# A conditioning map moved out of the FFNs into the first attention stage, with its scores spread

## The chip, the cores and the metric

The kernel runs on one core of one Trainium2 chip. The time is the device time of one execution in microseconds (us), smaller is better; a verdict compares the medians of runs. The engines that appear below: PE multiplies matrices, PEld loads its stationary operand, DVE, ACT and POOL work on vectors, SP issues the transfers.

## What is computed

One step of a two-layer trunk on 512 latent tokens and 128 context tokens, model width 1024. Both layers have a token mixer (layer 0: windowed attention, "mixer A"; layer 1: neighbourhood attention, "mixer B") and a gated FFN with a short convolution. In front of each of the four sub-layers the tokens are normalised and modulated by a shift and a scale, and behind it the result is gated; shift, scale and gate come from a condition vector by a linear map, one per layer:

```python
def adaln(cond, w_ada, b_ada):
    m = jax.nn.silu(cond) @ w_ada + b_ada
    return [t[:, None, :] for t in jnp.split(m, 6, axis=-1)]

    hs = modulate(rmsnorm(xs, norm_attn_w[i]), ms[0], ms[1])
    ...
    xs = xs + ms[2] * o_s
    hs = modulate(rmsnorm(xs, norm_ffn_w[i]), ms[3], ms[4])
    xs = xs + ms[5] * conv_ffn(hs, w_up[i], conv_w[i], conv_b[i], w_down[i])
```

`w_ada` is 1024 x 6144 in float32 for each layer, 25 MB. Since it depends on the condition alone, its product can be made at any time before its first use.

## The kernel before

The 640 tokens are five tiles of 128 (tile 4 is the context). Nearly every product is made in three passes of float32r halves ("hi" and "lo": an ACT copy and a subtraction, on POOL or DVE), so each weight that arrives is split first: `load_w` (line 130 the transfer, 161 the ACT copy `whi`, 164 the subtraction `wlo`).

**The conditioning map, "adaLN blocks".** Each layer's `w_ada` is cut into 12 blocks of 512 columns. A block is four transfers of 512 KB (`adst`, four buffers, so exactly one block), then two steps of the generator `ada_queue`. Its first step makes eight sums on PE (`ps_ada<-adst,cT`), copies the row out of PSUM (`adrow`: ACT, line 189, or DVE, line 191, by the flag `on_act`) and issues the next block's four transfers, which wait for these sums since they reuse the buffers. Its second step is `ada_done`: a few small PE products of `adrow` with a selection matrix, and a DVE operation into `mcol` or, for gates, a copy and a transfer to DRAM. Four of the 24 blocks are made at the start (`ada_first`). Before the change six are made in mixer A and fourteen in the FFNs: twelve in layer 0's and two in layer 1's, at the places that `ADA_UPS` lists among the 44 up-projections.

**Mixer A** runs in slots n = 3 to 20. A slot n has the scores of one pair of head group and query tile, the probability product of the pair before, and a share of the next group's projections. The order of the slot is written out as a string of letters in `SLOTS`, one for each piece: S is one head's score (two products into `ps_s`, which has two buffers, a DVE maximum with the mask, an ACT exponential `pexp`), V a step of the probability product (transposes `ps_p`, split by ACT and DVE into `ptr`, products `ps_o`), T a transposition of new queries and keys (`ps_tr`), Q a sixth-row piece of the projections (three products into `ps_mm`), O a piece of the output projection (`ps_op`), A one step of `ada_queue`. PE follows this order strictly. For the other engines and SP a scheduler places instructions within what the dependences allow; transfers on SP go out in the order so made, one queue, and one that waits holds those behind it.

**The start** follows two strings (`START`): x loads a token tile, n normalises and transposes it (`first_pre`), w loads weights, p and d are the first blocks' steps, f modulates a tile's half (`first_post`, lines 265 to 269), q a tile's projections.

**Row norms** (`norm_stat`, line 339, and `first_pre`, line 245) take the sum of squares of a row, then `rsqrt`: one DVE operation (303), logarithm and exponential on ACT (305, 308), four one-element DVE operations (310 to 313) of which three read two tensors, and a DVE multiplication of the whole row (339). They stand before each FFN: there the output projection's last tiles are normed and transposed (`ps_nt`), modulated (365, 367), split (375, 376) and fed to the first up-projections (`ps_up`). The order there is the string `OPROJ`.

**The FFN** (`ffn`) goes over 22 pairs of up-projections (`ps_up`) with convolution and gate (lines 920 to 948) and, in groups, down-projections (`ps_dn`).

Of the kernel before, what the change touches and what calls it, by code (L numbers as in the profile page):

```python
# [18 lines left out]
P = 128  # L19
# [10 lines left out]
SLOTS = {"A3": "SSQSTST", "A4": "SASATQSVTSQVQVQVQV", "A19": "SSVTSVSVTVV",  # L30
         "AT": "SOOSOOSVOSVOTVOOVTOVOOVOOSVOSVOSVOOSVOOVOOVOOSVOSVOSVOSVOOVOOOVOOVO",
         "a0": "SQSQSVTSVQTQVQVQVQVQ", "a1": "SQSQSTVSTVQTQVQVQVQVQ", "a2": "SQSQSVTSVQTQVQVQVQQ",
         "a3": "VQQTSQSVTSQSQQQQ", "a4": "QSTQSQSTSVQVQVQVQQV",
# [20 lines left out]

ADA_UPS = (0, 1, 3, 4, 6, 7, 8, 9, 11, 12, 14, 15, 17, 18, 20, 21, 23, 24, 26, 27, 29, 30, 32, 33), (0, 1, 3, 4)
# [8 lines left out]
class Trunk:  # L66
# [189 lines left out]
    def first_post(self, xT, hT, h, t, lo_eng):  # L256

        nc = self.nc
        A = self.abA[(0, 0)]
        j = 1 if t == 4 else 0  # L260
        sl = slice(t * P, (t + 1) * P)
        for c in range(4):
            f = 4 * h + c
            v = xT[h][:, c, sl]
            i = nc.vector.tensor_scalar(v, v, A[:, j, f:f + 1], self.mcol[0][:, j, f:f + 1], op0=OP.mult, op1=OP.add)
            self.tc.keep_in_program_order(i)
        v, d = xT[h][:, :, sl], [hT[p][h][:, :, sl] for p in range(2)]
        nc.scalar.activation(d[0], v, AF.Copy)  # L268
# [64 lines left out]
    def norm_stat(self, x, pool):  # L333

        nc = self.nc
        xn = pool.tile([P, D], F32, name="xn", tag="xn", bufs=self.xn_bufs)
        ss = self.sm.tile([P, 1], F32, name="nss", tag="nss")
        nc.scalar.activation(xn, x, AF.Square, accum_out=ss)
        nc.vector.tensor_scalar(xn, x, self.rsqrt(ss, 1, D), None, op0=OP.mult)  # L339
        return xn  # L340
# [585 lines left out]
    def ffn(self, l, hT, xs, groups, first, ahead, after):  # L926
# [3 lines left out]
        for gi, n in enumerate(groups):  # L930
            gh = self.ap.tile([P, 4, T], F32R, name="gh", tag="act")
            gl = self.ap.tile([P, 4, T], F32R, name="gl", tag="act")
            for k in range(n):
                zz = []
                for ff in (f + k, f + k + NF):
# [8 lines left out]
                    after("up")  # L944
# [19 lines left out]
def body(nc, tc, I, O):  # L964
    with ExitStack() as top:
# [16 lines left out]
        with ExitStack() as c1:  # L982
# [4 lines left out]
            for w in START[0].split():  # L987
# [8 lines left out]
                elif w[0] == "w":  # L996
                    W.append(k.load_w(I["wqa"][0, i], 768, k.wp, None, (sp, "load", 12)))
# [8 lines left out]
        with c2:  # L1006
            k.mp = k.pool(c2, "mixa", side="right")
            k.qT_bufs, k.pexp_bufs = 3, 4
            steps = k.ada_queue([(0, n) for n in range(4, 10)], True, "p", 3)
# [23 lines left out]
            for w in START[1].split():  # L1033
# [4 lines left out]
                elif w[0] == "f":  # L1038
                    k.first_post(xT, hT, 1, i - 10, nc.gpsimd if i > 12 else nc.vector)
# [9 lines left out]
            for n in range(3, 21):  # L1049
# [127 lines left out]
def finish_layer(k, l, wo, of, xsrc, cw):  # L1177
    nc = k.nc
    with ExitStack() as c:
        k.xp = k.pool(c, f"x{l}", side="right")  # L1180
        k.fp = k.pool(c, f"ffn{l}", side="right")
        if l == 1:
            k.adp = k.pool(c, "ada2", side="right")
# [17 lines left out]
        k.ada_next = k.ada_tiles(l, 10)  # L1201
# [115 lines left out]
        k.ffn(l, hT, xs, (4, 4, 2, 4, 4, 4), first, ahead, after)  # L1317
# [78 lines left out]
```

## Time and profile before

| what | value |
|---|---|
| median of three runs | 1751.34 us (1751.18 to 1751.69) |
| the profiled execution | 1752.72 us, of which the span 1750.9 us |
| PE busy | 1634.8 us (93%) |
| DVE, ACT, POOL busy | 894.9, 759.6, 943.5 us |
| mean granted PE clock | 0.975 |
| moved by transfers | 184.86 MB |

The durations quoted below come from that one profiled execution. A line of the timeline gives the start and the length in us, the engine, the line of the kernel, what is written and read, and in square brackets the idle time ahead of it with what ended it. A line of a table of stretches gives the stretch and its length, then each engine's busy time with its instructions in brackets, then the granted clock of PE, the busy share of the transfer engines and GB/s. A line of the waits gives who waited for whom, us in total, times, and the longest. In names of rows, line numbers are those of the kernel before.

The stages by time: the start to about 82 us; mixer A's slots 3 to 19 to 295; the rest of mixer A with the output projection to 379; layer 0's FFN to 880; mixer B to about 1225; output projection and norms to 1283; layer 1's FFN to the end.

### The profile page before, as it was taken

The page shows a single profiled execution, that of the slowest core. Times are in us where ns is not written, and L with a number is a line of the kernel's source. Part 1 is how long each engine was busy: PE and PEld are TensorE (multiplying, and loading weights), DVE is VectorE, ACT ScalarE, POOL GpSimd, SP SyncE. Part 2 cuts the span into 40 slices and gives each one's busy share as a digit, 9 for nine tenths or more (in the row PEclk, how much of TensorE's full clock was granted, in tenths as well). Part 3 has the DMA queues.
Part 4 walks back from the last instruction along what each step waited for, and adds up shares of the span by engine and source line. Part 5 has one row for each costly group of instructions (what it writes and reads, how often), then busy time and mean ns, then how long its engine had stood idle before and what let it go on. Part 6 is the DMA issues. An engine that isn't in the chain of part 4 may idle for free.

```text
span 1750.9 us, 26310 instructions
## 1 busy us (share of the span) xinstructions
PE 1634.8 (93%) x9736; PEld 1460.2 (83%) x9736; DVE 894.9 (51%) x2147; ACT 759.6 (43%) x1697; POOL 943.5 (54%) x790
## 2 busy tenths in 40 slices
PE   6798888989999999999988999998999999999998
PEld 4666776778889888899978899987789999999997
DVE  4777787673333242333475667677653232432334
ACT  4465656454132222232355777776442232323231
POOL 1544445454454573556535767776455656746461
PEclk9799998999999999999999999999999999999999
DMA  8432222425243344231222211123533222213131
GB/s 315 150 120 81 97 89 89 159 84 203 99 181 109 111 142 145 97 124 56 65 101 73 78 54 49 61 91 116 200 109 97 74 84 74 84 61 97 49 97 61
DMA packets 74592, 184.86 MB, mean 106 GB/s; under 512 B 16200, under 2 KB 25672, under 8 KB 74464
## 3 DMA queue, kind: packets, MB, share of 16 engines
q1 hardware_dynamic: 74464, 183.18, 31.2%
q8 instruction: 77, 1.26, 0.3%
q14 instruction: 51, 0.42, 0.1%
HBM read 171.32 MB, written 14.12 MB: 106 GB/s over the span
## 4 chain that ended last, share of the span: by engine, by line
PE 78%; DVE 11%; ACT 5%; DMA 2%; issue 2%; POOL 1%; SPq 0%; DVEq 0%; ACTq 0%; POOLq 0%
PE ps_up L136 35%; PE ps_dn L136 19%; PE ps_mm L136 10%; PE ps_ada L136 3%; PE ps_s L136 2%; PE ps_o L136 2%; PE ps_op L136 2%; PE ps_p L142 2%; PE ps_tr L142 1%; ACT pexp L641 1%; PE ps_nt L142 1%; DVE ps_s L636 1%; DVE xn L339 1%; DVE rs_r L313 1%; ACT whi L161 1%
## 5 line engine op out<-in xcount | busy, mean ns | idle before, releaser
L136 PE MATMUL ps_up<-hF,whi 128*128 128x320 f32 x2688 | 602.4, 311 | 5.1 <-POOL hF L376 5.1
L164 POOL TENSOR_TENSOR wlo<-wst,whi 128x1024 fp32r<-128x1024 f32 (+3 forms) x192 | 418.7, 2186 | 242.6 <-ACT whi L161 238.4
L136 PEld LDWEIGHTS ps_up<-hF,whi 128*128 128x128 f32 x2688 | 454.8, 189 | 25.4 <-issue 6.8
L136 PE MATMUL ps_up<-hF,wlo 128*128 128x320 f32 x1344 | 416.5, 311 | 0.0
L161 ACT ACTIVATE whi<-wst 128x1024 fp32r<-128x1024 f32 (+3 forms) x195 | 186.5, 962 | 437.1 <-PE ps_dn L136 160.5
L136 PEld LDWEIGHTS ps_up<-hF,wlo 128*128 128x128 f32 x1344 | 253.7, 189 | 4.9 <-issue 2.6
L922 DVE SCALAR_TENSOR_TENSOR z<-ps_up,convc,z 128x511 f32<-128x511 f32 (+1 forms) x176 | 95.8, 544 | 288.1 <-ACT z L920 284.3
L463 POOL TENSOR_TENSOR x<-x,xtmp 128x512 f32<-128x512 f32 x100 | 129.3, 1297 | 147.9 <-DVE xtmp L462 147.8
L462 DVE TENSOR_TENSOR xtmp<-ps_dn,gate 128x512 f32<-128x512 f32 x120 | 81.8, 689 | 241.7 <-PE ps_dn L136 238.8
L136 PE MATMUL ps_mm<-whi,hB 128*128 128x384 f32 x580 | 181.5, 352 | 9.5 <-DVE rs_r L327 9.5
L136 PE MATMUL ps_dn<-whi,gh 128*128 128x512 f32 x440 | 173.0, 393 | 1.8 <-DVE xtmp L462 1.6
L136 PE MATMUL ps_dn<-wlo,gh 128*128 128x512 f32 x440 | 172.2, 391 | 0.0
L136 PE MATMUL ps_dn<-whi,gl 128*128 128x512 f32 x440 | 169.8, 390 | 0.0
L136 PE MATMUL ps_mm<-whi,hA 128*128 128x384 f32 x320 | 114.5, 388 | 13.1 <-ACT hA L268 9.6
L948 POOL TENSOR_TENSOR gl<-z,gh 128x640 fp32r<-128x640 f32 x44 | 69.2, 1572 | 92.3 <-ACT gh L947 92.3
L136 PEld LDWEIGHTS ps_mm<-whi,hB 128*128 128x128 f32 x580 | 109.0, 191 | 11.7 <-ACT vb L513 8.9
L920 ACT ACTIVATE z<-ps_up,convc 128x640 f32<-128x640 f32 x88 | 76.9, 874 | 70.0 <-PE ps_up L136 69.9
L923 DVE SCALAR_TENSOR_TENSOR z<-ps_up,convc,z 128x511 f32<-128x511 f32 (+1 forms) x176 | 96.6, 549 | 5.6
L136 PE MATMUL ps_mm<-wlo,hB 128*128 128x384 f32 x290 | 98.6, 340 | 0.0
L136 PEld LDWEIGHTS ps_dn<-whi,gh 128*128 128x128 f32 x440 | 82.6, 188 | 17.8 <-DVE xtmp L462 3.5
L136 PEld LDWEIGHTS ps_dn<-whi,gl 128*128 128x128 f32 x440 | 82.3, 188 | 17.2
L136 PEld LDWEIGHTS ps_dn<-wlo,gh 128*128 128x128 f32 x440 | 82.6, 188 | 13.7
(210 smaller groups left out, 2950.1 us busy)
## 6 DMA issues: line engine op xcount, KB each, us to landing
adst<-in_wada_dram SPq DMA_DIRECT2D x96, 512.0 KB
wst<-in_wup_dram SPq DMA_DIRECT2D x78, 512.0 KB
wst<-in_wdown_dram SPq DMA_DIRECT2D x44, 512.0 KB
wst<-in_wqb_dram SPq DMA_DIRECT2D x29, 384.0 KB
wst<-in_wqa_dram SPq DMA_DIRECT2D x16, 384.0 KB
xd<-xring SPq DMA_DIRECT2D x20, 256.0 KB
x<-xd SPq DMA_DIRECT2D x10, 512.0 KB
wst<-in_woa_dram SPq DMA_DIRECT2D x8, 384.0 KB
```

The source lines that it names most:

```text
L136: i = self.nc.tensor.matmul(out, lhsT, rhs, start=start, stop=stop)
L142: i = self.nc.tensor.transpose(out, in_, idn)
L161: i = nc.scalar.activation(hi, st, AF.Copy)
L164: (lo_eng or nc.gpsimd).tensor_tensor(lo, st, _f(hi), OP.subtract)
L313: nc.vector.tensor_tensor(r, l, u, OP.mult)
L339: nc.vector.tensor_scalar(xn, x, self.rsqrt(ss, 1, D), None, op0=OP.mult)
L462: nc.vector.tensor_tensor(tmp, ps, gate[:, j, sl], OP.mult)
L463: (nc.gpsimd if pool_add else nc.vector).tensor_tensor(x[:, sl], x[:, sl], tmp, OP.add)
L920: nc.scalar.activation(z, u, AF.Identity, scale=w[:, 1:2], bias=w[:, 3:4])
L922: nc.vector.scalar_tensor_tensor(z[:, a + 1:b], u[:, a:b - 1], w[:, 0:1], z[:, a + 1:b], op0=OP.mult, op1=OP.add)
L923: nc.vector.scalar_tensor_tensor(z[:, a:b - 1], u[:, a + 1:b], w[:, 2:3], z[:, a:b - 1], op0=OP.mult, op1=OP.add)
L948: nc.gpsimd.tensor_tensor(gl[:, k], zz[0], _f(gh[:, k]), OP.subtract)
```

## The change

Three edits are made at once.

1. `ADA_UPS`, and with it every block in the FFNs, goes. Mixer A's queue now holds 20 blocks: the rest of layer 0 and all of layer 1. Each slot string has two A (one block), and the four S, which stood near the slot's front, are spread over it. All rows of these blocks are now copied by ACT.
2. In the start, the string is reordered (f03, f13 and f14 come earlier), the last two modulations of the second half go to ACT (`on_act`) with the lo part on DVE, and two weights' lo parts go from POOL to DVE.
3. The row norms use `rsqrt_row`: three one-element DVE operations that read one tensor and take the other operands as per-row scalars.

```diff
-SLOTS = {"A3": "SSQSTST", "A4": "SASATQSVTSQVQVQVQV", "A19": "SSVTSVSVTVV",
+SLOTS = {"A3": "SAQSATSTS", "A4": "SASATQVTSQVQVSQVQV", "A19": "SASATSVTSVVSVVO",
...
-         "a0": "SQSQSVTSVQTQVQVQVQVQ", "a1": "SQSQSTVSTVQTQVQVQVQVQ", "a2": "SQSQSVTSVQTQVQVQVQQ",
+         "a0": "SAQQASVQTSVQVSQTVQVQVQ", "a1": "SAQQASTVQTSVQVSTQVQVQVQ", "a2": "SAQQASVQTSVQVSQTVQVQQ",
...
-ADA_SLOTS, ADA_PLACES = (6, 9, 11, 14), (1, 3)
-START = ("... f00 f01 f02 q0 p p p p q1 n3 p p p p w2 w3 d q2 n4 f03 f04 d s1 q3 q4",
-         "f10 f11 f12 c q0 l0 l1 q1 t f13 l2 l3 q2 a f14 Q Q Q Q t t q3 A Q Q A t t q4")
+START = ("... f00 f01 f02 q0 p p p p q1 n3 f03 p p p p w2 w3 d q2 n4 f04 q3 d s1 q4",
+         "f10 f11 f12 f13 f14 c q0 l0 l1 q1 t l2 l3 q2 a Q Q Q Q t t q3 A Q Q A t t q4")
...
-ADA_UPS = (0, 1, 3, 4, 6, 7, 8, 9, 11, 12, 14, 15, 17, 18, 20, 21, 23, 24, 26, 27, 29, 30, 32, 33), (0, 1, 3, 4)
...
-        nc.vector.tensor_scalar(xn, x, self.rsqrt(ss, 1, D), None, op0=OP.mult)
+        nc.vector.tensor_scalar(xn, x, self.rsqrt_row(ss, D), None, op0=OP.mult)
...
+            sc, sh = A[:, j, f:f + 1], self.mcol[0][:, j, f:f + 1]
+            if on_act:
+                nc.scalar.activation(v, v, AF.Identity, scale=sc, bias=sh)
+            else:
+                i = nc.vector.tensor_scalar(v, v, sc, sh, op0=OP.mult, op1=OP.add)
...
+    def rsqrt_row(self, ss, d):
+        nc = self.nc
+        a, l, u, r = (self.sm.tile([P, 8], F32, name=f"rs_{v}", tag=f"rs_{v}")[:, 0:1] for v in "alur")
+        nc.vector.tensor_scalar(a, ss, 1.0 / d, EPS, op0=OP.mult, op1=OP.add)
+        i = nc.scalar.activation(l, a, AF.Ln)
...
+        nc.scalar.activation(l, l, AF.Exp, scale=-0.5)
+        nc.vector.tensor_scalar(u, l, l, a, op0=OP.mult, op1=OP.mult)
+        nc.vector.tensor_scalar(u, u, -0.5, 1.5, op0=OP.mult, op1=OP.add)
+        nc.vector.tensor_scalar(r, u, l, None, op0=OP.mult)
+        return r
...
-                    W.append(k.load_w(I["wqa"][0, i], 768, k.wp, None, (sp, "load", 12)))
+                    W.append(k.load_w(I["wqa"][0, i], 768, k.wp, nc.vector if i < 2 else None, (sp, "load", 12)))
...
-            steps = k.ada_queue([(0, n) for n in range(4, 10)], True, "p", 3)
+            steps = k.ada_queue([(0, n) for n in range(4, 12)] + [(1, n) for n in range(12)], True, "p", 3)
...
-                    k.first_post(xT, hT, 1, i - 10, nc.gpsimd if i > 12 else nc.vector)
+                    k.first_post(xT, hT, 1, i - 10, nc.vector, i > 12)
...
-        blocks = [(l, 10), (l, 11)] + [(1, n) for n in range(10) if l == 0]
-        steps = k.ada_queue(blocks, False, "dn", 2)
-        ups_done = iter(range(44))
-        def after(kind, *args):
-            if kind == "up":
-                if next(ups_done) in ADA_UPS[l]:
-                    next(steps)
-            else:
-                last(*args)
```

How this moves instructions, at three places. The first is PE in mixer A, from the first score of slot n = 10 on (`pexp` are exponentials, `hA` the modulated tokens, `adst` a block's columns, `adrow` its row). Before:

```order
L136 MATMUL ps_s<-kTa,qTa 128x512 x2
L136 MATMUL ps_mm<-whi,hA_100 128x384
L136 MATMUL ps_mm<-wlo,hA_100 128x384
L136 MATMUL ps_mm<-whi,hA_102 128x384
L136 MATMUL ps_s<-kTa,qTa 128x512 x2
L136 MATMUL ps_mm<-whi,hA_100 128x384
L136 MATMUL ps_mm<-wlo,hA_100 128x384
L136 MATMUL ps_mm<-whi,hA_102 128x384
L136 MATMUL ps_s<-kTa,qTa 128x512 x2
L142 MATMUL ps_p<-ident,pexp 128x128 x4
L142 MATMUL ps_tr<-identr,kd 128x128 x2
L136 MATMUL ps_s<-kTa,qTa 128x512 x2
```

and now:

```order
L132 MATMUL ps_s<-kTa,qTa 128x512 x2
L132 MATMUL ps_ada<-adst,cT 32x512 x8
L132 MATMUL ps_mm<-whi,hA_100 128x384
L132 MATMUL ps_mm<-wlo,hA_100 128x384
L132 MATMUL ps_mm<-whi,hA_102 128x384
L132 MATMUL ps_mm<-whi,hA_100 128x384
L132 MATMUL ps_mm<-wlo,hA_100 128x384
L132 MATMUL ps_mm<-whi,hA_102 128x384
L132 MATMUL ps_ada<-sel,adrow 128x2 x4
L132 MATMUL ps_s<-kTa,qTa 128x512 x2
L138 MATMUL ps_p<-ident,pexp 128x128 x4
```

Where four scores stood within twelve rows there are now two, with a whole block between them.

The second is DVE ahead of layer 0's FFN, at the norms of the last two token tiles. Before:

```order
L303 TENSOR_SCALAR rs_a<-nss 128x1
L310 TENSOR_TENSOR rs_u<-rs_l 128x1
L311 TENSOR_TENSOR rs_u<-rs_u,rs_a 128x1
L312 TENSOR_SCALAR rs_u<-rs_u 128x1
L313 TENSOR_TENSOR rs_r<-rs_l,rs_u 128x1
L339 TENSOR_SCALAR xn<-x,rs_r 128x1024
L310 TENSOR_TENSOR rs_u<-rs_l 128x1
L311 TENSOR_TENSOR rs_u<-rs_u,rs_a 128x1
L312 TENSOR_SCALAR rs_u<-rs_u 128x1
L313 TENSOR_TENSOR rs_r<-rs_l,rs_u 128x1
L339 TENSOR_SCALAR xn<-x,rs_r 128x1024
```

and now:

```order
L299 TENSOR_SCALAR rs_a<-nss 128x1
L304 TENSOR_SCALAR rs_u<-rs_l,rs_a 128x1
L305 TENSOR_SCALAR rs_u<-rs_u 128x1
L306 TENSOR_SCALAR rs_r<-rs_u,rs_l 128x1
L353 TENSOR_SCALAR xn<-x,rs_r 128x1024
L304 TENSOR_SCALAR rs_u<-rs_l,rs_a 128x1
L305 TENSOR_SCALAR rs_u<-rs_u 128x1
L306 TENSOR_SCALAR rs_r<-rs_u,rs_l 128x1
L353 TENSOR_SCALAR xn<-x,rs_r 128x1024
```

Four operations between exponential and row multiplication have become three, and none of them reads two tensors.

The third is ACT at the end of the start (`xT` are transposed tokens, `hA` their hi part). Before:

```order
L268 ACTIVATE hA_99<-xT_111 128x4x128
L268 ACTIVATE hA_100<-xT_112 128x4x128
L543 ACTIVATE kd<-kva 128x128
L513 ACTIVATE va<-kva 128x64 x2
L268 ACTIVATE hA_99<-xT_111 128x4x128
L161 ACTIVATE whi<-wst 128x768
L268 ACTIVATE hA_100<-xT_112 128x4x128
```

and now:

```order
L268 ACTIVATE hA_99<-xT_111 128x4x128
L263 ACTIVATE xT_112<-xT_112,mcol_83,abA_261 128x128 x8
L527 ACTIVATE va<-kva 128x64
L557 ACTIVATE kd<-kva 128x128
L527 ACTIVATE va<-kva 128x64
L268 ACTIVATE hA_100<-xT_112 128x4x128 x2
L157 ACTIVATE whi<-wst 128x768
```

Eight modulations now stand on ACT ahead of the first hi parts of the second half.

More of the change, by code (lines that the diff above doesn't have):

```diff
@@ L28 @@
 TU = 47
[L30 to L33 removed]
+SLOTS = {"A3": "SAQSATSTS", "A4": "SASATQVTSQVQVSQVQV", "A19": "SASATSVTSVVSVVO",
+         "AT": "SOOSAOAOSVOSVOTVOOVTOVOOVOOSVOSVOSVOOSVOOVOOVOOSVOSVOSVOSVOOVOOOVOOVO",
+         "a0": "SAQQASVQTSVQVSQTVQVQVQ", "a1": "SAQQASTVQTSVQVSTQVQVQVQ", "a2": "SAQQASVQTSVQVSQTVQVQQ",
+         "a3": "SAQQASVQTSQVQSTQQQ", "a4": "SAQTAQSVQTSVQVSQVQVQQ",
          "b0": "SVQQSQHPPVQQQQVQ", "b1": "VQHPSQQSHPQQVQQHV", "b2": "QHVQSPSQHQVQVQHPQ",
@@ L254, in first_pre, with first_post @@
                 nc.vector.tensor_copy(dst, ps)
-    def first_post(self, xT, hT, h, t, lo_eng):
+    def first_post(self, xT, hT, h, t, lo_eng, on_act=False):
         nc = self.nc
@@ L264, in first_post @@
             v = xT[h][:, c, sl]
-            i = nc.vector.tensor_scalar(v, v, A[:, j, f:f + 1], self.mcol[0][:, j, f:f + 1], op0=OP.mult, op1=OP.add)
-            self.tc.keep_in_program_order(i)
+            sc, sh = A[:, j, f:f + 1], self.mcol[0][:, j, f:f + 1]
[3 more added lines that the diff above has]
+                i = nc.vector.tensor_scalar(v, v, sc, sh, op0=OP.mult, op1=OP.add)
+                self.tc.keep_in_program_order(i)
         v, d = xT[h][:, :, sl], [hT[p][h][:, :, sl] for p in range(2)]
@@ L293, in rsqrt @@
         return out[0]
+    def rsqrt_row(self, ss, d):
[3 more added lines that the diff above has]
+        i = nc.scalar.activation(l, a, AF.Ln)
+        if self.act_pin is not None:
+            self.dep(i, self.act_pin)
+        nc.scalar.activation(l, l, AF.Exp, scale=-0.5)
[3 more added lines that the diff above has]
+        return r
     def rsqrt_steps(self, ss, n, d, out):
@@ L338, in norm_stat @@
         nc.scalar.activation(xn, x, AF.Square, accum_out=ss)
-        nc.vector.tensor_scalar(xn, x, self.rsqrt(ss, 1, D), None, op0=OP.mult)
+        nc.vector.tensor_scalar(xn, x, self.rsqrt_row(ss, D), None, op0=OP.mult)
         return xn
@@ L924, in conv, with ffn @@
         return z
-    def ffn(self, l, hT, xs, groups, first, ahead, after):
+    def ffn(self, l, hT, xs, groups, first, ahead, end):
         nc, fp = self.nc, self.fp
@@ L943, in ffn @@
                     zz.append(self.conv(u[0], ff, fp))
-                    after("up")
                 silu = nc.scalar.activation(zz[0], zz[0], AF.Silu)
@@ L948, in ffn @@
                 nc.gpsimd.tensor_tensor(gl[:, k], zz[0], _f(gh[:, k]), OP.subtract)
-            last = gi == len(groups) - 1
-            if last:
+            if gi == len(groups) - 1:
                 self.pin_exp(silu)
@@ L955, in ffn @@
                 gate = self.load_gate(l, 1)
-            if last:
-                after("last", (gh, gl), W, gate)
+            if gi == len(groups) - 1:
+                end((gh, gl), W, gate)
                 continue
@@ L1066, in body @@
                     order = SLOTS[f"A{n}" if n < 5 or n == 19 else f"a{n % 5}"]
-                    if n in ADA_SLOTS:
-                        a, b = ADA_PLACES
-                        order = order[:a] + "A" + order[a:b] + "A" + order[b:]
                     run(gens, order, only="QTO")
@@ L1181, in finish_layer @@
         k.fp = k.pool(c, f"ffn{l}", side="right")
-        if l == 1:
-            k.adp = k.pool(c, "ada2", side="right")
         k.psf = ExitStack()
@@ L1200, in finish_layer @@
         hT = k.new_hT(f"hF{l}")
-        k.ada_next = k.ada_tiles(l, 10)
         k.convc = k.fp.tile([P, 44, 4], F32, name="convc")
@@ L1249, in finish_layer @@
         k.chain = False
-        blocks = [(l, 10), (l, 11)] + [(1, n) for n in range(10) if l == 0]
-        steps = k.ada_queue(blocks, False, "dn", 2)
-        ups_done = iter(range(44))
-        def after(kind, *args):
-            if kind == "up":
-                if next(ups_done) in ADA_UPS[l]:
-                    next(steps)
-            else:
-                last(*args)
         def last(g, W, gate):
-            for _ in steps:
-                pass
             if l == 0:
@@ L1315, in last @@
             k.chain = False
-        k.ffn(l, hT, xs, (4, 4, 2, 4, 4, 4), first, ahead, after)
+        k.ffn(l, hT, xs, (4, 4, 2, 4, 4, 4), first, ahead, last)
         if l == 1:
```

2 lines of the change are left out of this document (1 added, 1 removed).

## The prediction

> **What bounds the kernel now.** I read the page first: busy time of the engines, the slices, the granted clock.
>
> ```profile
> PE 1634.8 (93%) x9736; PEld 1460.2 (83%) x9736; DVE 894.9 (51%) x2147; ACT 759.6 (43%) x1697; POOL 943.5 (54%) x790
> PE   6798888989999999999988999998999999999998
> PEclk9799998999999999999999999999999999999999
> ```
>
> PE is the bound: 93% busy, every other engine near half. Its eights and sevens lie in the first nine slices (some 44 us each), its nines in the FFNs, so the same PE work costs less in the one than in the other. A table of stretches puts numbers on that:
>
> ```profile
> 82.40:100.80 18.40, 16.17 (x84) 10.09 (x84) 13.57 (x47) 12.79 (x39) 8.56 (x12) 0.91 0.46 163
> 100.80:274.10 173.30, 149.61 (x855) 123.61 (x854) 130.51 (x361) 104.06 (x301) 74.67 (x107) 0.94 0.26 85
> 274.10:295.50 21.40, 13.90 (x56) 9.40 (x55) 15.34 (x39) 14.79 (x41) 16.12 (x17) 0.76 0.45 153
> 295.50:355.00 59.50, 56.30 (x311) 46.70 (x309) 40.82 (x76) 25.16 (x57) 26.01 (x26) 1.00 0.45 146
> 399.99:860.64 460.65, 460.61 (x2829) 413.01 (x2830) 160.80 (x271) 134.12 (x152) 250.51 (x135) 1.00 0.36 125
> 1289.87:1716.90 427.03, 427.03 (x2602) 401.18 (x2602) 145.63 (x247) 131.98 (x149) 245.24 (x132) 1.00 0.26 83
> ```
>
> The rows are slots 3 and 4, slots 5 to 17, slots 18 and 19, the rest of mixer A's attention, and the two FFNs from the same first products to the same last ones (below). In the slots PE idles 23.7 of 173.3 us at a granted clock of 0.94; in the FFNs it idles 0.04 us. The waits of the slots' stretch name the cause of the idling:
>
> ```profile
> PE ps_s L136 <- ACT pexp L641: 13.5, 16, 3.0
> PE ps_o L136 <- DVE ptr L676: 6.2, 13, 1.0
> ```
>
> 13.5 us in 16 waits: the third score finds both `ps_s` buffers taken until an exponential has read one. 6.2 us: products of the probabilities wait for their split operand. Both are latencies that work of PE's own, placed between, would cover.
>
> **The change part by part.** The sum is made against the profiled execution, 1752.72 us; the runs' median lies 1.4 below it.
>
> *FFNs, 14 blocks out.* Both FFN rows start at the same products, of equal length:
>
> ```profile
> 399.99 10.75 PE ps_up L136 x72
> 1289.87 10.75 PE ps_up L136 x72
> 183.84 1.98 PE ps_ada L136 x16
> 187.83 1.05 PE ps_ada L136 x8
> 398.13 1.85 PE ps_ada L136 x16
> ```
>
> Layer 0's stretch holds 11 blocks' sums and 12 second steps, layer 1's one and two: 10 blocks more, and 460.65 - 427.03 = 33.6 us more, 3.4 each. In mixer A a block's records are 1.98 + 1.05 = 3.03 us. PE is full in both FFNs, so nothing is hidden: 14 x 3.37 = **-47.2**. The lower bound is the records alone, 14 x (1.85 + 0.85) = -38 (sums as in layer 0's FFN, 0.85 an estimate for a second step without waits, below the 1.05 shown). I take the difference of the stretches, since it contains what lies between records.
>
> *Slots 5 to 17, nine blocks in, scores spread.* PE is busy 149.6 us; of this about 9.0 is lost to half clock (0.06 of the clock over the stretch), so the work at full clock is 140.6, with four blocks. Nine more cost 9 x 3.03 = 27.3, so 167.9 us for 13 slots. What idling remains? Two slots that hold a block now show it:
>
> ```profile
> 183.30:198.50 15.20, 13.68 (x91) 10.49 (x90) 11.14 (x32) 8.40 (x25) 5.38 (x9) 1.00 0.62 226
> 198.50:210.10 11.60, 10.82 (x70) 9.48 (x68) 8.53 (x25) 8.39 (x25) 5.82 (x9) 1.00 0.00 0
> ```
>
> 1.5 us in the one with a block, 0.8 in a good one without, both at full clock. I take 1.2 per slot, 15.6 in all: 183.5 against 173.3, **+10.2**. Ends: no idling at all, 167.9, -5.4; nothing absorbed, +27.3.
>
> *Slots 3 and 4, 18 and 19, the last stage.* Slots 3 and 4 get one block more (+3.0), less about 3.2 of idle and half clock that it fills, and face the block buffer: there is one, so sums that follow each other closely wait for a transfer. I put 5 on that (transfer of some 8 us against 5 to 6 us of PE work between the sums, an estimate from the next rows): **+4.8**. Slots 18 and 19 idle 7.5 us at 0.76: two blocks of 6.06 fit, **0**. The last stage is 56.30 of 59.50 busy: two blocks cost their price, **+6.1**.
>
> *Transfers in the slots.* A block is issued only when the one before has been summed:
>
> ```profile
> 185.70 1.75 SPq L130 DMA_DIRECT2D adst<-in_wada_dram  x4
> 190.00:196.00 6.00, 5.94 (x41) 5.14 (x39) 4.98 (x17) 5.00 (x14) 2.33 (x5) 1.00 0.90 355
> SPq L130 <- POOL wlo L164: 86.9, 13, 41.3
> L189 ACT ACTIVATE adrow<-ps_ada x6: 578/592/598, 78.1 to 224.8; 98x512 f32<-98x512 f32 x6
> ```
>
> 2.1 MB at 355 GB/s are 5.9 us, and from issue to the end of the traffic it is 8 to 10.3. With 2 us of sums a round is 10 to 12.2 us, and a slot would last 183.5 / 13 = 14.1. So it fits, with 1.9 us to spare at worst. The third row (start to slot 20) says what may eat that: SP, one queue in order, waited for POOL's `wlo` 13 times, 6.7 us in the mean, the longest 41.3. Weights stand on the same queue. I take **+3**; ends 0 and the price of rival D.
>
> *Norms ahead of the FFNs.* In layer 0:
>
> ```profile
> 379.70 0.48 DVE L310 TENSOR_TENSOR rs_u<-rs_l 128x1 f32<-128x1 f32 x1
> 380.21 1.22 DVE L311 TENSOR_TENSOR rs_u<-rs_u,rs_a 128x1 f32<-128x1 f32 x1
> 381.47 0.16 DVE L312 TENSOR_SCALAR rs_u<-rs_u 128x1 f32<-128x1 f32 x1
> 381.66 1.59 DVE L313 TENSOR_TENSOR rs_r<-rs_l,rs_u 128x1 f32<-128x1 f32 x1
> 383.35 1.11 DVE L339 TENSOR_SCALAR xn<-x,rs_r 128x1024 f32<-128x1024 f32 x1
> 384.38 2.33 DVE L310 TENSOR_TENSOR rs_u<-rs_l 128x1 f32<-128x1 f32 x1
> 386.75 2.34 DVE L311 TENSOR_TENSOR rs_u<-rs_u,rs_a 128x1 f32<-128x1 f32 x1
> 389.31 1.00 DVE L313 TENSOR_TENSOR rs_r<-rs_l,rs_u 128x1 f32<-128x1 f32 x1
> 390.41 0.75 DVE L339 TENSOR_SCALAR xn<-x,rs_r 128x1024 f32<-128x1024 f32 x1
> 383.88 5.19 POOL L164 TENSOR_TENSOR wx<-ust,wx 128x1024 fp32r<-128x1024 f32 x2
> 384.61 1.06 PE L142 MATMUL ps_nt<-ident,xn 128*128 128x128 f32 x8 [1.26 <-DVE xn L339]
> 391.31 0.63 PE L142 MATMUL ps_nt<-ident,xn 128*128 128x128 f32 x4 [2.11 <-DVE xn L339]
> 392.50 1.12 PE L142 MATMUL ps_nt<-ident,xn 128*128 128x128 f32 x4 [0.56 <-DVE xn L365]
> 393.65 1.50 ACT L367 ACTIVATE xn<-ps_nt,mcol,abA 128x128 f32<-128x128 f32 x4 [0.55 <-PE ps_nt L142]
> 390.00:395.00 5.00, 3.13 (x14) 2.92 (x15) 3.61 (x10) 1.98 (x5) 1.56 (x2) 0.73 0.00 0
> ```
>
> An operation of one element takes 0.16 us (L312), but with two tensors up to 2.34, as long as the POOL subtractions beside it (two in 5.19 us). Six of them cost 9.0 us where 1.0 would do, so both rows come about 8 us earlier in sum. PE waited 1.26 + 2.11 + 0.56 = 3.9 us there, and lost about 1.6 to the lower clock after (0.73 over 390 to 395, the same below 1 up to 400): 5.5 at most per FFN. The two multiplications of whole rows remain, and the modulations behind them are next in line. I take 4.5 twice, since layer 1's chain has the same form and like lengths: **-9.0**; ends 0 and -11.
>
> By the Trainium skill, "SBUF — State Buffer", section "SBUF: two separate sides", DVE and POOL share a port pair, which a DVE operation with two SBUF inputs, or in a mode that uses two ports, takes for its whole length, and the other engine waits. The trace agrees with the first half (0.16 against 2.34); it would leave this term as it is, but the row multiplication of 1024 elements could still wait one POOL subtraction, 2.6 us: if that came on the path each time, the term would be -9.0 + 2 x 2.6 = -3.8.
>
> *The start.* One gap stands between the tokens' first and second half:
>
> ```profile
> 70.09 0.69 PE L136 MATMUL ps_mm<-whi,hA 128*128 128x384 f32 x1 [4.05 <-ACT hA L268]
> 70.00:73.50 3.50, 3.08 (x8) 2.57 (x9) 2.43 (x7) 0.03 (x1) 2.13 (x2) 0.50 0.00 0
> 83.00:85.00 2.00, 1.28 (x9) 0.93 (x7) 2.00 (x7) 1.65 (x6) 2.00 (x2) 1.00 0.61 248
> ```
>
> PE waited 4.05 us for ACT's hi part, and 3.5 us at half clock follow (0.50), which is 1.7 us lost there, and I allow 1 for the slow rise after it; earlier modulations could take up to 7 in all. But eight modulations on ACT, 0.37 us each (by the four of L367, of this size, above), now stand ahead of the hi parts, 3 us. I take **-3**, ends -7 and +3. Behind it DVE and ACT are busy nearly throughout (83 to 85 us: 2.00 and 1.65 of 2.00) and PE is what idles, so the two `wlo` moved to DVE bring little: 0.
>
> The other `rsqrt_row` places (mixer B's norms) have PE work on both sides: 0. ACT's 14 extra row copies, 0.59 us each (the row of L189), stand beside 104.06 us busy of 173.30 and are covered by ACT's own idling; without that cover they are in the slots' 1.2 us.
>
> Sum: -47.2 + 10.2 + 4.8 + 0 + 6.1 + 3 - 9.0 - 3 = -35.1, so 1717.6 by the profiled execution, and 1716 by the median.
>
> **The rivals.**
>
> *B: the slots absorb nothing.* ACT and DVE set the slots' pace, and a block only shifts the wait to another score. For it: the three splits `ptr` per slot keep their 6.2 us whatever stands between scores, and ACT gets the row copy on top. Against: the slot at 183.3 has 15.20 us with 1.5 idle. The slots' term becomes +27.3: 1716 + 17 = 1733.
>
> *C: the new one-element operations wait for POOL like the old.* They take per-row scalars from memory, which may count as second inputs. For it: no row shows a one-element operation with a scalar from memory beside POOL. Against: the row multiplication, which takes such a scalar, ran 0.75 to 1.11 us, less than the two-tensor ones. The -9.0 goes: 1725.
>
> *D: transfers come late, slower than before.* The next block's transfers stand on SP behind a weight's transfer that waits for its buffer, that is for POOL's `wlo`; the sums stand in PE's order, so PE stops until they land. At the 6.7 us of a wait in the mean less 1.9 of slack it is 4.8 us per block, which eats 35.1 from 7.3 blocks on; at ten blocks it is 1716 + 48 = 1764. For it: 86.9 us of such waits now, with six blocks. Against: the traffic of slots 5 to 17 was 0.26 of the engines' time, and one of those 13 waits is 41.3 us, so the others are 3.8.
>
> **How the numbers follow.** Forecast 0.55: 1716, its own range 1702 (no idling left in the slots) to 1731 (the ends of the norms and slots 3 and 4 against me). B 0.20, C 0.10, D 0.09, others, mostly between these, 0.06. To leave out no more than 2 in 10, the range goes from 1700 to 1742: B and C are in it, D is not. A difference under 0.2%, 3.5 us, is no change that these runs can tell. B and C are faster too; D is slower: faster 0.88, same 0.03, slower 0.09.
>
> **What would show it.** Layer 0's FFN from first to last product of the same names: 427 us as layer 1's. Slots 5 to 17: about 183 us, PE over 90% busy, clock near 1.00, PE's waits for `pexp` mostly gone; B if these 13 slots take 200 us. `ps_ada` products waiting for a transfer more than 1 us at more than a few slots would be D. One-element operations of 0.15 to 0.2 us in the row chain and PE's waits for `xn` gone would show the norms right; operations over 1 us there are C. In the start the gap before the second half's first `ps_mm` should fall under 2 us. I am wrong if the FFNs keep part of the 33.6 us, or the last stage grows by more than 6.

## The result, and the profile after

The changed kernel took 1721.03 us in the median (four runs, 1718.12 to 1722.9) against 1751.26 of the kernel before (four runs, 1748.7 to 1751.69): the ratio is 0.983, with a 95% interval of 0.981 to 0.985. That is 30.2 us less. The profiled execution was the shortest of the four, 1718.12 us with a span of 1716.3, 34.6 us less than the profiled execution before; the stages below come from it. A second profile, taken later on another chip and called "again" here, has a span of 1722.9; where the two differ, both are given.

The page of the changed kernel, as shown of before:

```profile
PE 1619.1 (94%) x9736; PEld 1453.7 (85%) x9736; DVE 862.6 (50%) x2109; ACT 771.5 (45%) x1719; POOL 939.4 (55%) x786
PE   6789989999999999999969999998999999999998
PEclk9899999999999999999989999999999999999999
```

Most of the eights of the slots have become nines. A six has come up in the slice at 858 to 901 us, where mixer B begins: this is new.

The table of stretches of the changed kernel: slots 3 and 4, slots 5 to 17, slots 18 and 19, the first 59.5 us of the last stage of mixer A (as long as the row of before, but not the same work), layer 0's FFN between the same products as before, and mixer B from its first projection to its first output projection. Behind them is mixer B in the kernel before.

```profile
79.20:106.60 27.40, 21.59 (x107) 11.90 (x106) 15.62 (x53) 13.79 (x41) 8.62 (x13) 0.94 0.50 189
106.60:285.80 179.20, 165.11 (x1035) 125.75 (x1034) 126.26 (x367) 108.63 (x308) 75.36 (x103) 0.98 0.53 190
285.80:310.70 24.90, 21.56 (x117) 14.95 (x116) 16.44 (x49) 18.04 (x47) 19.12 (x22) 0.86 0.85 302
310.70:370.20 59.50, 57.94 (x328) 44.69 (x327) 40.79 (x76) 25.78 (x58) 24.45 (x24) 1.00 0.61 204
411.12:833.88 422.76, 422.76 (x2583) 400.54 (x2582) 144.80 (x243) 133.99 (x152) 250.94 (x137) 1.00 0.24 74
869.91:1151.16 281.25, 256.57 (x1627) 247.57 (x1625) 181.50 (x619) 192.41 (x620) 185.96 (x246) 0.97 0.21 63
```

```profile
896.78:1173.08 276.30, 255.16 (x1627) 245.79 (x1626) 181.22 (x620) 192.85 (x620) 186.50 (x246) 0.98 0.21 64
```

Layer 0's FFN between the same products is 422.76 us now against 460.65. Thirteen slots hold thirteen blocks and take 5.9 us more than with four. Slots 3 and 4 take 9.0 more. Mixer B takes 5.0 more, though nothing in it was meant to change.

PE's waits in the slots of the changed kernel (79 to 310 us; who waited for whom, us in total, times, longest), and behind them SP's greatest (0 to 340 us):

```profile
PE ps_ada L132 <- ACT adrow L185: 9.9, 7, 2.7
PE ps_o L132 <- DVE ptr L690: 6.3, 7, 1.3
PE ps_ada L132 <- DMA adrow<-in_b_ada_dram: 3.9, 1, 3.9
PE ps_ada L132 <- DMA adst<-in_wada_dram: 1.3, 3, 0.9
PE ps_s L132 <- ACT pexp L655: 0.8, 2, 0.5
```

```profile
SPq L126 <- PE ps_ada L132: 120.3, 16, 13.7
SPq L126 <- POOL wlo L160: 25.2, 10, 8.2
```

The scores no longer wait for exponentials (13.5 us before over slots 5 to 17 alone, 0.8 now). A new wait has their place: a block's second step waits for ACT's copy of the row. The blocks' transfers themselves cost PE 1.3 us in all.

At mixer B's begin (860 to 935 us) PE's greatest waits are, in the changed kernel:

```profile
PE ps_mm L132 <- DVE rs_r L341: 7.0, 1, 7.0
PE ps_nt L138 <- DVE xn L353: 6.3, 2, 3.5
```

The second row was there before as well (7.9). The first one was not: the second projection tile of mixer B waits 7.0 us for the last operation of a row norm that reads the first tile's PSUM bank.

And the chain ahead of layer 0's FFN, on DVE, in the changed kernel:

```profile
397.56 0.27 DVE L304 TENSOR_SCALAR rs_u<-rs_l,rs_a 128x1 f32<-128x1 f32 x1
397.86 0.15 DVE L305 TENSOR_SCALAR rs_u<-rs_u 128x1 f32<-128x1 f32 x1
398.06 0.21 DVE L306 TENSOR_SCALAR rs_r<-rs_u,rs_l 128x1 f32<-128x1 f32 x1
398.38 1.42 DVE L353 TENSOR_SCALAR xn<-x,rs_r 128x1024 f32<-128x1024 f32 x1
```

Three operations take 0.63 us where four took up to 5.8. PE's waits for `xn` in front of both FFNs are at most 0.4 us each.

Four questions follow. Is the new wait in mixer B worth what it seems, and which edit made it? Are the second steps' waits a matter of place or of the pace of ACT and DVE? What do the three edits bring apart? And are the blocks cheap because they fill holes, or because the scores are spread?

### The profile page after: what moved, and what is told of

Read it like the earlier page. It is cut to its first block, busy times and chain, and to the rows that moved or that the text cites. A ratio compares the mean times of both kernels' runs of the same rounds, so it can differ in the third digit from the quotient of the medians.

```text
span 1716.3 us, 26311 instructions
## 1 busy us (share of the span) xinstructions
PE 1619.1 (94%) x9736; PEld 1453.7 (85%) x9736; DVE 862.6 (50%) x2109; ACT 771.5 (45%) x1719; POOL 939.4 (55%) x786
## 5 line engine op out<-in xcount | busy, mean ns | idle before, releaser
L132 PE MATMUL ps_mm<-whi,hA 128*128 128x384 f32 x320 | 111.0, 376 | 8.3 <-ACT hA L268 6.3
```

Of the source, the lines that this page charges most:

```text
L132: i = self.nc.tensor.matmul(out, lhsT, rhs, start=start, stop=stop)
```

## The experiments

All are compared with the kernel before in runs of their own chip. An interval of a ratio is about 0.0015 either way, that is 2.6 us. Three chips were used in turn; the kernel before took 1750.27, 1750.91 and 1750.58 us on them, so differences between runs of different chips are taken directly. Line numbers are those of the changed kernel unless a row says another.

**The changed kernel again**, the base of the next three.

> The changed kernel once more, on the chip on which its three variants run, so that they have a base. The runs so far gave 1718.1 to 1722.9 us; the profiled one was the shortest of them. If the spread is a property of the kernel, the median is again 1720 to 1722, and a profile shows which stage it moves in.

Measured: 1721.82 us, ratio 0.9835 (0.9820 to 0.9850). The spread is there again, 1719.65 to 1724.68 us. The slots up to the first output projection took 235.35 us against 230.8 in the shorter profile, with nearly the same waits. Slot 13 shows how (the first row from the shorter profile, the second from this one):

```profile
218.20:231.20 13.00, 10.52 (x70) 7.99 (x69) 10.26 (x25) 7.58 (x21) 7.33 (x10) 1.00 0.68 244
```

```profile
219.20:234.70 15.50, 13.12 (x69) 10.81 (x68) 9.88 (x27) 7.75 (x21) 7.29 (x10) 0.78 0.56 205
```

In both, the second step waits 2.38 us for `adrow`. In one the granted clock stays at 1.00, in the other it falls to 0.78 for the slot.

**The bank.** The pools of mixer B take PSUM banks in the order in which their tags first come up. One tile more in front shifts the projections' pair by one bank:

```diff
             k.psp = k.pool(c2, "psb", space=PSUM)
+            k.psp.tile([P, 512], F32, name="ps_o", tag="o", bufs=1)
```

> The changed kernel, with mixer B's second projection tile in another PSUM bank than the first. Theory 1 (the bank): the 7.0 us in which PE waits at 880.6 us is the second tile waiting for the bank that the first one's row norm still reads; before the change the two lay in different banks. Then that wait falls below 1.5 us, the stretch from the first ps_mm of mixer B to its first ps_op from 281 to about 276 us, and the time by 5 to 6 us, to about 1715. Theory 2 (something later ends last anyway, the weights that arrive at 898.7 to 906.7 us): the wait moves behind, and the time falls by less than 2 us.

Measured: 1715.61 us, ratio 0.9794 (0.9779 to 0.9808), 6.2 us less than the base. The stretch of mixer B and the waits in it:

```profile
872.42:1146.72 274.30, 255.03 (x1627) 245.69 (x1626) 181.22 (x619) 192.22 (x620) 185.80 (x246) 0.98 0.22 64
```

```profile
PE ps_nt L138 <- DVE xn L353: 6.2, 2, 3.5
PE ps_tr L138 <- ACT hsb L779: 2.7, 1, 2.7
...
PE ps_mm L132 <- DVE rs_r L341: 1.0, 1, 1.0
```

The wait for `rs_r` at 880 us fell from 7.0 to 1.0, and nothing later takes more than a part of it back. Theory 1 holds.

**Later second steps**, in slots 5 to 18 (one of the five strings; the others alike):

```diff
-"a0": "SAQQASVQTSVQVSQTVQVQVQ"
+"a0": "SAQQSVQTASVQVSQTVQVQVQ"
```

> The changed kernel, with the second step of each block in slots 5 to 18 placed behind the next score, two or three pieces later. Theory 1 (the row copy): PE's waits at the second steps, 10.0 us in slots 5 to 18, are ACT's copy of the row standing behind an exponential; given two pieces more of cover, 8 of the 10 us go and 1 to 3 of half clock with them: 9 us less, about 1712. Theory 2 (ACT and DVE set the pace of a slot): PE waits as long for another exponential or another split operand, and the time stays within 2 us.

Measured: 1712.02 us, ratio 0.9779 (0.9766 to 0.9793), 9.8 less than the base. PE's waits in the slots (78 to 302 us):

```profile
PE ps_o L132 <- DVE ptr L690: 6.1, 14, 0.9
PE ps_ada L132 <- DMA adrow<-in_b_ada_dram: 3.9, 1, 3.9
PE ps_o L132 <- ACT ptr L689: 2.9, 3, 1.2
...
PE ps_ada L132 <- ACT adrow L185: 0.6, 1, 0.6
```

9.9 us of waits for `adrow` became 0.6. The part of `ptr` that DVE splits costs what it did, but 2.9 us of waits for ACT's part of it are new. The stretch from the first score to the first output projection, in the changed kernel and here:

```profile
79.20:310.00 230.80, 207.56 (x1253) 152.03 (x1252) 158.32 (x466) 139.97 (x394) 102.40 (x137) 0.96 0.56 202
```

```profile
78.40:302.00 223.60, 206.11 (x1253) 148.72 (x1252) 160.84 (x466) 138.55 (x394) 102.29 (x137) 0.98 0.58 208
```

PE idles 17.5 us here and 23.2 in the changed kernel (23.9 again): of the 9.3 us some 6 are a gain in idling, and the rest of the 9.8 shows as shorter PE time, at a higher clock. Theory 1 holds in the main, with a part of theory 2: the copy of the row stood on ACT behind an exponential, which stood behind DVE. In slot 6 of the changed kernel the timeline of ACT, with PE's second step behind it, shows the queue:

```profile
123.80 0.58 ACT L655 ACTIVATE pexp<-ps_s,anm 128x384 f32<-128x384 f32 x1 [3.27 <-DVE anm L650]
...
125.24 0.42 ACT L624 ACTIVATE qd<-t1a 128x256 fp32r<-128x256 f32 x1 [0.77 <-DVE t1a L618]
...
125.77 0.58 ACT L185 ACTIVATE adrow<-ps_ada 98x512 f32<-98x512 f32 x1
126.39 1.05 PE L132 MATMUL ps_ada<-sel,adrow 98*128 98x2 f32 x8 [2.67 <-ACT adrow L185]
```

The sums were done at 122.5 us. ACT then idled 3.27 us in front of an exponential whose maximum was late, and only afterwards copied the row. (A copy on DVE in place of ACT was not tried.)

**Both.**

> Both edits together. If both causes are as in theory 1 their gains add, since they lie 600 us apart: 14 to 15 us less than the changed kernel, about 1706. If either falls, the sum is what the two single runs gave.

Measured: 1705.41 us, ratio 0.9738 (0.9724 to 0.9752), 16.4 less than the base: the two gains add (6.2 + 9.8). This is the best kernel found.

**The old row norms**, the rest as changed:

```diff
-self.rsqrt_row(ss, D)
+self.rsqrt(ss, 1, D)
```

> The changed kernel with the old row norms (four one-element operations, three of them with two tensors). Theory 1 (they wait for POOL): PE's waits for xn ahead of the two FFNs come back, 3.9 and 2.7 us, with the lower clock behind them; each FFN's first products take 5 us longer, and mixer B's norms 1 to 2: 10 to 12 us slower than the changed kernel. Theory 2 (rival C of the prediction, or a chain that is hidden now that the blocks are gone): within 3 us of it.

Measured: 1721.80 us, ratio 0.9828 (0.9812 to 0.9845): no difference to the base. By the total, theory 2. By the trace, neither as written. The chain in front of layer 0's FFN is back as it was:

```profile
407.00 2.34 DVE L324 TENSOR_TENSOR rs_u<-rs_l 128x1 f32<-128x1 f32 x1
409.38 2.33 DVE L325 TENSOR_TENSOR rs_u<-rs_u,rs_a 128x1 f32<-128x1 f32 x1
...
413.94 0.63 PE L138 MATMUL ps_nt<-ident,xn 128*128 128x128 f32 x4 [2.12 <-DVE xn L353]
```

The stretch of mixer B with the old norms:

```profile
878.18:1153.38 275.20, 255.00 (x1626) 245.64 (x1625) 181.26 (x620) 193.03 (x620) 186.20 (x246) 0.98 0.22 64
```

The first 200 products of layer 0's FFN, here and in the base:

```profile
399.35:438.00 38.65, 33.45 (x217) 32.47 (x216) 22.31 (x36) 19.42 (x34) 23.74 (x15) 0.96 0.19 64
```

```profile
398.90:434.54 35.64, 32.96 (x217) 32.55 (x216) 15.22 (x34) 19.35 (x34) 24.28 (x15) 0.95 0.20 70
```

They take 38.65 us against 35.64, those of layer 1's FFN 40.13 against 35.58: 7.6 us lost. But mixer B takes 275.20 against 281.53, 6.3 us gained: the wait of 7 us is not there. So it was the new row norm, not the removal of the blocks, that brought it. Where the built program places its tiles says how: with the old norms, the two transposes of the last token tile in front of layer 0's FFN take the pair of banks `dn` in the order 1, 0, with the new ones in the order 0, 1. (That the scheduler takes the one it reckons free first would explain it; this was not tried.) From there on all tiles of that pair alternate the other way round, and the first projection tile of mixer B, which is one of them, lies in bank 0 instead of 1, just where the second one begins.

**The old row norms with the bank edit.** If that is so, the edit that gained 6.2 us must now cost as much.

> The kernel with the bank edit and the old row norms. With the old norms the scheduler gives the two last tokens' transposes the FFN's pair of banks in the other order, so the bank edit, which took the collision away with the new norms, makes it here. Theory 1 (the collision is all that hid the norms' worth): the kernel is slower than the one with the bank edit alone (1715.6) by 7.5 us of norms and 6.5 of collision, about 1729, and slower than the one with old norms alone (1721.8) by 6 to 7. Theory 2 (mixer B's wait depends on when the norms end and not on the bank): no wait of 7 us in mixer B, and 1721 to 1723.

Measured: 1728.73 us, ratio 0.9879 (0.9863 to 0.9896), 13.1 us slower than with the bank edit alone and 6.9 slower than with the old norms alone. Among PE's waits at mixer B's begin it is there again:

```profile
PE ps_mm L132 <- DVE rs_r L341: 7.1, 1, 7.1
```

Theory 1 holds, to within half a microsecond. The built programs agree. The banks of mixer B's first and second projection tile are 1 and 0 in the kernel before, 0 and 0 in the changed one, 0 and 1 with the bank edit, 1 and 0 with the old norms, and 1 and 1 with both. PE waits 7.0 to 7.9 us where the two are equal, and about 1 us or less where they differ. The row norms are worth about 7 us where the bank does not take them back (1728.73 - 1721.82 = 6.9 with the collision in both kernels, 1721.80 - 1715.61 = 6.2 with it in neither).

**The old start.**

```diff
-... q1 n3 f03 p p p p w2 w3 d q2 n4 f04 q3 d s1 q4", "f10 f11 f12 f13 f14 c q0 l0 l1 q1 t l2 l3 q2 a ...
+... q1 n3 p p p p w2 w3 d q2 n4 f03 f04 d s1 q3 q4", "f10 f11 f12 c q0 l0 l1 q1 t f13 l2 l3 q2 a f14 ...
-k.first_post(xT, hT, 1, i - 10, nc.vector, i > 12)
+k.first_post(xT, hT, 1, i - 10, nc.gpsimd if i > 12 else nc.vector)
```

(and the two lo parts of `wqa` back on POOL)

> The changed kernel with the old start (order, modulations and lo parts as before). Theory 1: the first score comes at 82.4 us again and not at 79.2, and all after it 3 us later: 3 us slower. Theory 2: the sums of slot 3 wait for their block's transfer and bias row whatever the start does (the changed kernel idles 5.6 us in slot 3), so what the start gains is lost there, and the time stays within 1.5 us.

Measured: 1720.80 us, ratio 0.9829 (0.9814 to 0.9843), no difference. The first score comes at 83.0 us and not at 79 us, but slot 3 is short (the first row with the old start, the second of the changed kernel):

```profile
83.00:91.70 8.70, 7.38 (x38) 3.01 (x36) 5.79 (x21) 5.22 (x19) 3.58 (x5) 1.00 0.64 222
```

```profile
79.20:94.20 15.00, 9.43 (x37) 3.66 (x35) 7.77 (x24) 6.00 (x19) 5.46 (x8) 0.89 0.45 168
```

Slot 4 even begins earlier, at 91.7 against 94.2 us. Theory 2 holds by the time: what the start gains is waited for in slot 3, though a run below shows that slot 3 is not the whole reason. In slot 3 of the changed kernel PE stands 3.9 us for the bias row of a gate block, which SP issues only behind two results that are late (SP's timeline):

```profile
87.36 0.36 SPq L622 DMA_DIRECT2D out_dram<-kvo  x1
87.82 0.37 SPq L621 DMA_DIRECT2D out_dram<-kvo  x1
88.29 0.26 SPq L126 DMA_DIRECT2D adrow<-in_b_ada_dram  x1
88.64 1.76 SPq L126 DMA_DIRECT2D adst<-in_wada_dram  x4
```

**Scores spread, blocks where they were.**

```diff
-"A3": "SAQSATSTS", "a0": "SAQQASVQTSVQVSQTVQVQVQ", ...  # twenty blocks here
+"A3": "SQSTSTS", "a0": "SQQSVQTSVQVSQTVQVQVQ", ...      # six here, fourteen in the FFNs
```

> The changed kernel with its blocks where they were (six in mixer A, fourteen in the FFNs) and the scores still spread. The FFNs must give back 45 us, the last stage of mixer A saves 4, mixer B's bank wait 5. Theory 1 (the holes are filled by the blocks): the slots from first score to first output projection take 213 us as before the change and not 231, and the kernel is 18 us slower than the changed one, about 1738. Theory 2 (spreading the scores alone takes the waits away, and the blocks then cost their full price of 36 us): 195 us and about the same time as the changed kernel, 1720.

Measured: 1728.19 us, ratio 0.9877 (0.9850 to 0.9903), 6.4 slower than the base, with intervals that touch, and between the two theories. Slots 5 to 17 with four blocks:

```profile
97.10:254.80 157.70, 143.10 (x844) 118.47 (x843) 123.74 (x357) 102.51 (x298) 74.03 (x102) 0.97 0.29 93
```

157.7 us against 173.3 before the change: spreading alone takes 15.6 us away. The changed kernel's 179.2 (182.0 again) is 21.5 to 24.3 more for nine blocks, 2.4 to 2.7 each of their 3.03. So for the slots theory 2 is nearer. The total went wrong on the bank: I had counted 5 us for mixer B's wait going away with the blocks back in the FFNs; it stayed (7.3 us), since the new norms make it. This run and the one with the old norms are what turned me from the blocks to the norms as its cause. With that wait on both sides, moving fourteen blocks is worth those 6.4 us.

**Blocks moved, scores not spread.**

```diff
-"a0": "SAQQASVQTSVQVSQTVQVQVQ"
+"a0": "SAQSAQSVTSVQTQVQVQVQVQ"
```

> The changed kernel with the letters of slots 5 to 18 as before the change (scores near the slot's front) and the two steps of a block put in at the second and fourth place, as six blocks had them. Theory 1 (blocks fill the holes in any order): within 4 us of the changed kernel. Theory 2 (without spreading, PE still waits for the third and fourth exponential, some 1.5 us a slot with the lower clock behind it): 13 slots by 1.5 is 20 us slower, about 1740.

Measured: 1725.09 us, ratio 0.9851 (0.9837 to 0.9866), 3.3 slower than the base, with intervals that touch. Slots 5 to 17:

```profile
106.10:294.40 188.30, 174.37 (x1072) 130.86 (x1071) 133.36 (x373) 114.07 (x318) 80.52 (x111) 0.97 0.53 188
```

Fifteen us more than before the change for nine blocks that cost 27.3 of PE's time: here the holes are filled. So theory 1 holds, and the two edits are in large part substitutes: 15.6 us go by spreading and some 12 by blocks, but together they take 21 away (27.3 - 5.9), 18.6 in the second profile. The total says the same. Each with the new start and the new norms, spreading without moving a block is 22.7 us faster than the kernel before (1750.91 to 1728.19), moving without spreading 25.8 (to 1725.09), and both 28.5 (1750.27 to 1721.82).

**Slot 3 without its block**, on top of both good edits; the block goes to the last stage:

```diff
-"A3": "SAQSATSTS", "AT": "SOOSAOAOSVOSVOTVOOVTO...
+"A3": "SQSTSTS",   "AT": "SOOSAOAOSVOSVOTAVOOVATO...
```

> The kernel with both edits (bank, later second steps), and the block of slot 3 made later, among the output projections of the last stage. Theory 1 (slot 3 waits for transfers: its sums for the block, its second step for the bias row, which stands on SP behind other transfers): slot 3 falls from 14.6 us to about 5, the last stage grows by the block's 3 us: 6 us less, about 1699. Theory 2 (the wait goes to the block of slot 4, whose transfer then is the late one): slot 4 grows by what slot 3 loses, and the time rises by 0 to 3 us.

Measured: 1706.97 us, ratio 0.9746 (0.9732 to 0.9761), no gain over 1705.41. Slot 3 did fall, from 14.8 to 5.4 us. Of the 9.4, 4.5 went in slots 4 to 18 (first row without slot 3's block, then with it) and 5 in the first quarter of the last stage, 23.5 against 18.4 for one block more:

```profile
84.10:281.70 197.60, 187.78 (x1156) 140.30 (x1156) 144.37 (x418) 125.19 (x355) 89.03 (x121) 0.97 0.56 196
297.50:321.00 23.50, 23.28 (x133) 15.00 (x132) 12.31 (x27) 8.79 (x20) 3.51 (x6) 1.00 0.60 210
```

```profile
94.40:287.50 193.10, 183.57 (x1161) 137.94 (x1161) 140.47 (x414) 123.86 (x351) 86.87 (x117) 0.99 0.57 200
302.90:321.30 18.40, 18.40 (x108) 13.34 (x108) 12.35 (x24) 8.09 (x19) 4.16 (x6) 1.00 0.48 166
```

Neither theory: the wait did not go to slot 4 (13.0 us against 12.8). The 4.5 us show as PE time at a lower granted clock (0.97 against 0.99), which differs from run to run as slot 13 showed; whether they belong to this kernel stays open.

**The same with the old start.**

> The same, with the old start. In the changed kernel the old start made no difference to the time (1720.8 against 1721.8), though the first score came 4 us later, since slot 3 then waited less. Theory 1 (the start's gain is lost in slot 3): with slot 3's waits gone the old start costs its 4 us: about 1703. Theory 2 (the gain is bounded by something else behind it): within 1.5 us of the same kernel with the new start.

Measured: 1708.81 us, ratio 0.9758 (0.9743 to 0.9772), 1.8 more than with the new start, within the intervals. In the profiles the first score is 4.5 us later, the last stage's begin 2.9 and the end 1.2. So even without slot 3's wait the start is worth 2 us or less; nearer to theory 2, and what takes the rest isn't shown.

**One lo part moved to DVE**, on the kernel without slot 3's block:

```diff
-k.norm_post(k.norm_tr(xn, t, dn=where == "d"), xn, l, 1, t, hT)
+k.norm_post(k.norm_tr(xn, t, dn=where == "d"), xn, l, 1, t, hT, lo_eng=nc.vector if t == 2 else None)
```

> The kernel with both edits and slot 3's block moved, and the lo halves of the third token tile in front of both FFNs on DVE and not on POOL. Theory 1 (what is left of the wait at the first up-projection, 2.7 us per FFN, is POOL's queue of weights' lo parts): 2 to 2.5 us go at each FFN, 4 to 5 in all. Theory 2 (the multiplications of whole rows on DVE are as late): the wait moves to them, and the time stays within 1.5 us.

Measured: 1715.59 us, ratio 0.9797 (0.9783 to 0.9812), 8.6 us slower. PE's waits in front of layer 0's FFN (386 to 427 us):

```profile
PE ps_nt L138 <- DVE xn L353: 5.6, 1, 5.6
PE ps_up L132 <- DVE hF L390: 1.0, 1, 1.0
```

The wait of 2.7 us for `hF` became 1.0, and the row multiplications, now behind two more operations on DVE, made PE wait 5.6. Theory 2's mechanism with a larger price than it gave: the wait moved and more than doubled.

## Why the prediction was right, and where it was wrong

The forecast was 1716 with a range from 1700 to 1742; 1721.03 lies in it, and in the likeliest case's own range. The sum was -35.1; the profiled pair gave -34.6 and the medians -30.2. That the sum came within 0.5 us of the pair is luck: single terms are off by up to 5 us, and the errors cancel. (The lower end of the likeliest case's range, 1702, was taken from the profiled 1717.6; from 1716 it is 1700.) Term by term, by the profiled pair:

| term | forecast | measured |
|---|---|---|
| fourteen blocks out of the FFNs | -47.2 | -45.2 |
| slots 5 to 17 | +10.2 | +5.9 (+8.7 again) |
| slots 3 and 4 | +4.8 | +9.0 |
| slots 18 and 19 | 0 | +3.5 |
| last stage of mixer A | +6.1 | +3.6 |
| transfers in the slots | +3 | in the rows above |
| norms ahead of the FFNs | -9.0 | -10.1 |
| start | -3 | -3.2, waited away in slot 3 |
| mixer B | 0 | +5.0 |

(The rows add to -31.5; the missing 3 lie at the borders of stages and behind mixer B, in shares of about 1. The last stage of mixer A is taken from its first output projection to the first up-projection: 80.8 us before, 84.4 now.) The FFN rows: from its first product to its last, layer 0's FFN fell by 44.4 us, layer 1's by 10.9. The first 200 products of each took 5.0 us less beyond the 4.66 us of block steps among them (from the start of each to that of the next product), which is put down to the norms; the rest is the blocks'.

**Right in size and cause: the FFNs and the norms.** With PE full, a block removed is a block gained, and the difference of two stretches with the same ends gave its price. The new one-element operations take 0.15 to 0.27 us where the old took up to 2.34, and PE's waits for `xn` in front of the FFNs fell to 0.4 us or less. Taken alone, by the runs with the old norms, the norms are worth 7.6 us in front of the FFNs and 6 to 7 in the time, so the table's 10.1 holds some 2.5 us whose cause stays open. The Trainium skill ("SBUF — State Buffer", "SBUF: two separate sides") said as much of the operations; its other half, that the row multiplication could still wait for POOL, agrees with one multiplication of 1.42 us in front of layer 0's FFN where others took 0.75 to 0.81. On the path each time, that wait would have left -3.8 of this term; 7.6 to 10.1 were measured, so it was not.

**Right in sum, by other shares: the slots.** The slots from 3 to 19 with their transfers were to cost 18.0; the first output projection came 17.3 us later after the first score (21.9 again). I had the holes filled by the blocks. The runs show two ways of filling them, and the change uses both. The waits that remain are of a new kind, and I had carried over 1.2 us of idling per slot as if of the old. What idles now is the second steps' wait for the row copy on ACT, 9.9 us, which I had dismissed with "covered by ACT's own idling". ACT does idle, 3.27 us in front of the copy; but it idles in order, with the copy queued behind the late exponential. That sentence was the wrong step, and putting it right took 9.8 us off the next kernel.

**Slots 3 and 4** were mis-sized, 4.8 against 9.0: I had put 5 us on the block's transfer. PE's waits for transfers came to 5.2, which is luck: the blocks' cost 1.3, and the bias row's, 0.26 us to issue but behind two late results on SP, cost 3.9, a transfer that I had not counted. Mis-sized were the block itself, whose products took 5.2 us more of PE's time in these slots and not 3.0, and the holes that it fills: the wait for exponentials gave back 1.6 us (2.1 to 0.5), and I had put 3.2 on idling and clock. The start's -3 was right as measured at the first score, and worth nothing in the end: slot 3 waits it away, and with slot 3's block gone it was still worth 2 us or less, for a reason that stays open.

**Mixer B is the term I did not have.** "The other `rsqrt_row` places have PE work on both sides: 0" looked at time only. A row norm with one operation fewer, and shorter ones, changed the order in which the scheduler gives out a pair of banks, and some 470 us later a product waits 7 us for a bank. So the edit whose mechanism I had right, and whose gain is plain in the trace, changed the kernel's time by nothing measurable (1721.80 with the old norms, 1721.82 with the new).

**The rivals.** B (the slots absorb nothing) fell: nine blocks cost 5.9 to 8.7 us and not 27.3, though its sign, the 6.2 us of `ptr`, is there nearly unchanged (6.3). With the scores spread already, nine blocks cost 21.5 to 24.3 us, so it is the spreading that made B wrong as much as the blocks. C (the one-element operations wait as before) fell by their durations. D (transfers late at most blocks) fell: SP's waits for POOL's `wlo` went down from 86.9 to 25.2 us, and PE waited 1.3 us for blocks; a queue in order cost time only at one bias row.

## What to carry to other kernels

Before an operation is called hidden because its engine idles, look at what it stands behind in that engine's order: idling in front of a late operation covers nothing queued after it. When two edits close the same holes, their gains don't add; run each alone before pricing the pair. And after any edit that changes what a scheduler places, compare which banks and buffers the same tiles got, far behind the edit too: a gain in one stage was paid back in full by a bank some 470 us later, and a line that moves the banks gave it back.

## What the runs showed of the hardware that was not expected

The same kernel with nearly the same waits ran 4.5 us apart over its slots in two executions, and its runs spread over 1718 to 1725 us. In slot 13 a wait of 2.38 us was followed by a clock of 1.00 in one execution and 0.78 in the other: 13.0 and 15.5 us. By the Trainium skill ("TensorE: Matmul & The Clock Gate", "Part 1: The HAM clock gate"), the clock is decided over free-running windows of some 3.4 us; a wait shorter than a window that meets one or another share of it, and so costs itself or twice itself, agrees with that, though no run here moved the phase on purpose. Waits of 2 to 3 us are thus dearer in the mean than they look in one profile: with the later second steps PE idled 5.8 to 6.4 us less in the slots, the time fell by 9.8, and the slots of that profile ran at a clock of 0.98 against 0.93 and 0.96. How much dearer, these few executions do not say.
